# Output projection of both layers as one 2x2 block product over all heads, in a two-layer decoder trunk

## The chip, the cores and the metric

The kernel runs on one core of a Trainium2 chip. A core has five instruction queues that run at the same time and wait for each other through semaphores: TensorE (PE, with its weight loads shown as PEld), VectorE (DVE), ScalarE (ACT), GpSimd (POOL) and SyncE (SP), which issues the DMAs. The metric is the device time of one execution in microseconds (us); smaller is better.

## The reference, cut to what matters

One sequence of 1024 tokens, width 1024, float32. Layer A is a retention layer of 4 heads (query and key width 256, value width 512), layer C a stick-breaking attention of 8 heads (128, value width 256) whose keys and values come from layer A's output. In both, all heads' outputs, gated, are concatenated to 2048 columns and multiplied by one 2048 x 1024 matrix; that is the output projection.

```python
# layer A
o = retention_chunkwise(q, k, v)                    # per head: (1024, 512)
o = (o - mu) * rsqrt(var + EPS)                     # over each head's 512 columns
o = merge_heads(o) * silu(g)                        # (1024, 2048)
y = o @ ret_w_out[i]                                # output projection, 2048 x 1024
h = x + rms_norm(y, ret_norm_post[i])
k_shared, v_shared = split(rms_norm(h, kv_norm) @ w_kv)
# layer C
z = einsum('bhqd,bhkd->bhqk', qb, k) * scale
log_not = where(causal, log_sigmoid(-z), 0)
suffix  = cumsum(log_not, axis=3, reverse=True) - log_not
weights = where(causal, exp(log_sigmoid(z) + suffix), 0)
o = merge_heads(einsum('bhqk,bhke->bhqe', weights, v)) * silu(g)
y = o @ sb_w_out[j]                                 # output projection, 2048 x 1024
h = h + rms_norm(y, sb_norm_post[j])
```

## The kernel before

*Arithmetic.* Every float32 operand of a matmul is split into a high and a low part: `split` writes the high part with ScalarE (L514) and the rest with VectorE (L515). `mm3` (L410) makes one product from three matmuls, high by high, high by low, low by high (L413, L414, L415). In the rows the tile `whl` holds split weights, `wraw` and `vo` raw ones, `xh` (and `oT`, `qk`, `AT`, `ko`) split activations.

*Tiling.* The tokens are two halves `t` of 512. The input projections of both layers are 2x2 block products already: 7 products (numbers 1, 2, 5, 6, 7, 3, 4) of half-size blocks where the plain way has 8, with sums and differences of the operands made by VectorE. They are cut into pieces by the class `Phase`, and `merge` deals the pieces of one job out among the steps of another.

*Heads.* Layer A has eight turns (t, head), layer C eight pairs (t, two heads), each in two half heads; I number these n = 0 to 15, where 0 to 7 are the first token half and 8 to 15 the second. In attention `rows` makes the scores of a half head: for each of four blocks of 128 queries (in the second half in two parts, the keys of the other half and the own ones) three matmuls into a `pz` bank, two sigmoids by ScalarE into a tile `A` (even n; `xh` for odd n) and a tile `sgn` (L1275, L1276), two triangular selections by POOL on the diagonal block (L1280, L1281), a running product by VectorE over all keys (L1283) and a multiply (L1284). `mix` then takes each block of 128 keys: PE turns it (L1311, four transposes, one for each block of queries, from the four tiles `A`), ScalarE and VectorE split it to `AT`, and PE multiplies it with V into two `po` banks. The scores of half head n + 1 are dealt out among the steps of `mix` of half head n. A gate multiplies `po` (L1339).

*Output projection, head by head.* `outs` (L427) multiplies one head's four blocks `oT` by that head's strip of weights, two blocks of the contraction at a time, for each of 8 blocks of 128 output columns; the result lies with the columns on partitions, and each head adds its part to a running sum `ys` in SBUF (L452 for the first head, L455 later). In attention's second half `out_t` does the same with the tokens on partitions. A head's projection (16 pieces) is dealt out among the steps of the next head, or the next pair: in retention by the loop in `layer_a`, in attention by this one, with the last pair's in `finish`:

```python
for n in range(2, 16):
    A = heads[n // 2]
    if n % 2 == 0:
        pre, out = heads[n // 2 - 1].out(ys, ...)
    ...
    merge(A.mix(n % 2), (out[8 * (n % 2):][:8], 0 if n % 2 else 1, 1), (rows_of(n + 1), 0, 1), (extra, 1, 1))
```

The sums are then normalised (`a_post`, `c_post`, `finish`) and x or h is added; attention's split weights are prepared by `w_out` and kept in DRAM (`w_d`).

*Order.* The code above only says which step depends on which. `arrange` (L101) collects every instruction of the engines, works out a latest time for each, places them one after the other on a model of the engines with its own prices (`place`), repeats this from the back (`justify`), keeps the best of five, and ties each engine's queue to that order. Within PSUM there are four kinds of bank, `ma`, `mb`, `z` and `o`, two of each; of `sgn` there are 2 tiles, of `AT` 3, of `whl` 3.

Of the kernel before, what the change touches and what calls it, by code (L numbers as in the profile page):

```python
# [13 lines left out]
F32 = mybir.dt.float32  # L14
# [4 lines left out]
D = 1024  # L19
# [47 lines left out]

def _time(s, chip):
# [32 lines left out]
def arrange(nc, tc, tag_of, bufs, banks, turns):  # L101
# [4 lines left out]
    for ins in nc.cur_bb.bb.instructions:  # L106
# [10 lines left out]
        reads = [(b.tensor.name, _cells(b)) for b in s.ins if type(b.tensor).__name__ == "Tile"]  # L117
        writes = [(b.tensor.name, _cells(b)) for b in s.outs if type(b.tensor).__name__ == "Tile"]
# [3 lines left out]
        for name, m in writes:  # L122
            s.before |= {o.k for o, n, w in last[name] if n & m}
        for name, m in reads:
            last[name].append((s, m, False))
# [183 lines left out]
def trunk(ctx, tc, xT, wts, gains, trig, ident_in, cols, last_gain, x_late, out):  # L309
# [62 lines left out]

    warm = sb.tile([128, 8], F32, name="warm")
# [25 lines left out]
    def unit(idx, gain=None):  # L399

        w = S("whl", [2, 1024], F32R)
        for c in range(2):
            o = 512 * c
            raw = raw_w()
            dma(raw, wts[idx, :, o:o + 512])
            for a, b, g in [(p[0] - o, p[1] - o, p[2]) for p in gain if o <= p[0] < o + 512] if gain else [(0, 512, None)]:
                split((w[:, 0, o + a:o + b], w[:, 1, o + a:o + b]), raw[:, a:b], g)
        return w

# [6 lines left out]

    def ahead(n, make):

        box = {}

        def get(u):
            if u < n and u not in box:
                box[u] = make(u)
            return box.get(u)
        return get

    def outs(weights, oT, ys, tags, first, y_d=None, acc=None, kept=None):  # L427


        box = {}  # L430
        get = ahead(4, weights)

        def chunk(j):
            c, half = divmod(j, 2)
            ng, b = divmod(c, 2)
            w = get(ng)
            if j % 4 == LEAD:
                get(ng + 1)
            if half == 0:
                box["p"] = PS(banks4[c % 4])  # L440
                if b == 0 and first:
                    ys.append(S(tags[ng], [2, 512]))
                if b == 0 and kept is not None:
                    kept.append(S("v", [2, 512]))
            p, y = box["p"], ys[ng][:, b]
            for e in (2 * half, 2 * half + 1):
                n = slice(256 * e + 128 * b, 256 * e + 128 * b + 128)
                mm3(p[:], w[:, 0, n], w[:, 1, n], oT()[e][:, 0, :], oT()[e][:, 1, :], e == 0, e == 3)
            if half == 0:
                return  # L450
            if first:
                A_.activation(y, p[:], AF.Copy)  # L452
                return
            f = y if acc is None else kept[ng][:, b] if kept is not None else S("f2", [512])[:]
            V.tensor_tensor(f, p[:], y, ALU.add)  # L455
            if acc is not None:
                if kept is None:
                    dma(y_d[c], f)
                sumsq(acc, f, c)

        return [lambda: get(0)], [lambda j=j: chunk(j) for j in range(16)]
# [13 lines left out]

    def sumsq(acc, src, c):
        if c == 0:
            acc.append(S("acc", [512]))
            A_.activation(acc[0][:], src, AF.Square)
        else:  # L480
            t = S("f2", [512])
            A_.activation(t[:], src, AF.Square)
            V.tensor_tensor(acc[0][:], acc[0][:], t[:], ALU.add)
# [40 lines left out]
    turned = out[0:512, :].rearrange("a (b t) -> (a b) t", b=2)  # L524
    straight = out[512:1024, :]
    ht_d = dr.tile([1024, 512], F32, tag="ht", name="ht")
    st_d = [[dr.tile([128, 512], F32, tag=f"st{h}{d}", name=f"st{h}{d}") for d in range(2)] for h in range(NH)]
    y_d = [[dr.tile([128, 512], F32, tag=f"y{t}{c}", name=f"y{t}{c}") for c in range(8)] for t in range(2)]
    h_d = [[DRAM(f"h{t}{c}", F32) for c in range(4)] for t in range(2)]
# [4 lines left out]
    w_d = [[[DRAM(f"w{p}{n}{i}", F32R) for i in range(2)] for n in range(4)] for p in range(NPAIR)]  # L534
# [12 lines left out]
    B, tabs = Ctx(), []  # L547

    def a_open():
# [58 lines left out]
        def sums(i):  # L608
            if i == 0:
                L.sum = S("small", [4])  # L610
            w = S("ko", [1024])
            dma(w[:], x_late[128 * i:128 * i + 128, :])
            A_.activation(w[:], w[:], AF.Square, accum_out=L.sum[:, i:i + 1])

# [8 lines left out]
    class Ret:  # L623
# [3 lines left out]

        def out(self, ys, acc=None, kept=None):
            return outs(lambda ng: unit(self.base + 12 + ng), lambda: self.oT, ys, ("AT", "AT", "AT", "A"), self.h == 0,
                        y_d[0], acc, kept)  # L630
# [140 lines left out]
        def gate(self):  # L771
            o = S("qk" if self.n % 2 else "oT", [4, 2, 512], F32R)
            self.oT = [o[:, e] for e in range(4)]
# [11 lines left out]

            return [lambda ib=ib: step(ib) for ib in range(4)]

    def a_post(t, y_d, acc, kept=None):

        box = {}  # L790

        def stat1():
            box["col"] = rstd_col(acc[0])
# [910 lines left out]
```

## Time and profile before

| | |
|---|---|
| median of 3 runs | 1626.89 us (1626.64 to 1629.45) |
| profiled execution: span from the first instruction to the last | 1625.3 us |
| what the median has beside that span | 1.6 us |
| PE busy | 1615.8 us (99%) |
| DVE, ACT, POOL busy | 1220.5, 804.1, 124.2 us |
| moved by DMA | 392.72 MB, mean 242 GB/s |

A row of the timeline reads: start, duration, engine, source line, operation, output tile<-input tiles, partitions x columns, count; in brackets the idle time before it and what ended it. A row of the groups has count, total busy time, mean duration in ns, idle time. A DMA row has the size of one and the median time from its issue to its landing.

### The profile page before, as it was taken

What the parts mean: (1) busy time and instruction counts of PE and PEld (TensorE: products, weight loads), DVE (VectorE), ACT (ScalarE), POOL (GpSimd) and SP (SyncE); (2) the same over time, 40 slices, a digit from 0 to 9 for tenths busy, and PEclk for the clock granted to TensorE, in tenths of its full rate; (3) what the DMA queues carried; (4) which work ended last, traced back from release to release, by engine and by line L of the source; (5) the groups of instructions that cost most, each with busy time, mean ns of one, the idle gap of its engine ahead of it and who ended that gap; (6) DMA issues with size and microseconds to landing.
All of it is one profiled execution on the core that took longest, in us unless ns stands there. A gap on an engine that the chain in (4) does not pass through costs nothing.

```text
span 1625.3 us, 22472 instructions
## 1 busy us (share of the span) xinstructions
PE 1615.8 (99%) x7619; PEld 1348.1 (83%) x7619; DVE 1220.5 (75%) x1957; ACT 804.1 (49%) x1535; POOL 124.2 (8%) x271
## 2 busy tenths in 40 slices
PE   9999999999999999999999999999999999999998
PEld 7888888888888888888888888888888888888887
DVE  8897866654668888887689877767649567878776
ACT  8653334433356555544356665557644433554442
POOL 0000000000022212211000000000001111011110
PEclk9999999999999999999999999999999999999999
DMA  9757755543387878784786788988337988869783
GB/s 318 240 166 261 246 205 197 207 143 122 119 265 254 305 251 281 235 293 144 238 292 207 263 310 300 333 291 300 132 123 236 332 300 322 289 221 326 260 244 93
DMA packets 194834, 392.72 MB, mean 242 GB/s; under 512 B 34976, under 2 KB 51488, under 8 KB 192160
## 3 DMA queue, kind: packets, MB, share of 16 engines
q1 hardware_dynamic: 194000, 390.23, 69.9%
q8 instruction: 60, 0.98, 0.2%
q10 hardware_dynamic: 720, 1.07, 0.2%
q14 instruction: 54, 0.44, 0.1%
HBM read 268.01 MB, written 123.21 MB: 241 GB/s over the span
## 4 chain that ended last, share of the span: by engine, by line
PE 98%; DVE 1%; issue 0%; ACT 0%; DMA 0%; SPq 0%; DVEq 0%; POOLq 0%; POOL 0%
PE pma L413 12%; PE pma L414 12%; PE pma L415 12%; PE pmb L413 9%; PE pmb L414 9%; PE pmb L415 9%; PE po L414 6%; PE po L415 6%; PE po L413 6%; PE pz L415 3%; PE pz L414 3%; PE pz L413 3%; PE pz L1311 2%; PE pz L783 1%; DMA A<-in_xT_dram 0%
## 5 line engine op out<-in xcount | busy, mean ns | idle before, releaser
L515 DVE TENSOR_TENSOR whl<-wraw,whl 128x512 fp32r<-128x512 f32 x266 | 176.1, 686 | 88.6 <-ACT whl L514 86.0
L514 ACT ACTIVATE whl<-wraw 128x512 fp32r<-128x512 f32 x266 | 156.2, 625 | 171.2 <-issue 65.6
L1283 DVE TENSOR_TENSOR_SCAN sgn<-sgn 128x128 f32<-128x128 f32 (+3 forms) x64 | 86.6, 1354 | 16.9 <-POOL sgn L1281 16.7
L515 DVE TENSOR_TENSOR AT<-pz,AT 128x512 fp32r<-128x512 f32 (+1 forms) x96 | 51.2, 552 | 51.9 <-ACT AT L514 51.6
L514 ACT ACTIVATE AT<-pz 128x512 fp32r<-128x512 f32 (+1 forms) x96 | 45.0, 491 | 70.7 <-PE pz L1311 69.7
L413 PE MATMUL pmb<-oT,whl 128*128 128x512 f32 x192 | 75.9, 395 | 0.0
L415 PE MATMUL pmb<-oT,whl 128*128 128x512 f32 x192 | 75.3, 392 | 0.0
L414 PE MATMUL pmb<-oT,whl 128*128 128x512 f32 x192 | 75.2, 392 | 0.0
L413 PE MATMUL pmb<-qk,whl 128*128 128x512 f32 x184 | 72.4, 394 | 0.0
L415 PE MATMUL pmb<-qk,whl 128*128 128x512 f32 x184 | 72.2, 392 | 0.0
L414 PE MATMUL pmb<-qk,whl 128*128 128x512 f32 x184 | 71.8, 390 | 0.0
L515 DVE TENSOR_TENSOR whl<-vo,whl 128x512 fp32r<-128x512 f32 x62 | 41.7, 689 | 35.1 <-ACT whl L514 35.0
L897 ACT ACTIVATE f<-pma 128x512 f32<-128x512 f32 x52 | 30.8, 595 | 49.8 <-PE pma L415 49.4
L514 ACT ACTIVATE whl<-vo 128x512 fp32r<-128x512 f32 x62 | 37.5, 624 | 33.6 <-PE pma L415 17.1
L413 PE MATMUL pma<-xh,whl 128*128 128x512 f32 x136 | 53.3, 392 | 0.0
L415 PE MATMUL pma<-xh,whl 128*128 128x512 f32 x136 | 53.1, 390 | 0.0
L414 PE MATMUL pma<-xh,whl 128*128 128x512 f32 x136 | 53.1, 390 | 0.0
L1280 POOL TENSOR_SCALAR_AFFINE_SELECT A<-A 128x128 f32<-128x128 f32 x32 | 12.0, 376 | 534.8 <-ACT A L1275 534.8
L920 ACT ACTIVATE wraw<-wraw,gn 128x256 f32<-128x256 f32 x102 | 45.4, 497 | 8.7 <-DMA wraw<-in_wts_dram 8.6
L1275 ACT ACTIVATE xh<-pz 128x512 f32<-128x512 f32 (+3 forms) x48 | 23.6, 492 | 50.9 <-PE pz L415 50.7
L1276 ACT ACTIVATE sgn<-pz 128x512 f32<-128x512 f32 (+2 forms) x96 | 46.7, 488 | 0.0
L690 POOL TENSOR_SCALAR_AFFINE_SELECT sc<-sc 128x256 fp32r<-128x256 f32 x16 | 10.8, 692 | 447.6 <-DVE sc L515 447.4
(578 smaller groups left out, 5142.3 us busy)
## 6 DMA issues: line engine op xcount, KB each, us to landing
wraw<-in_wts_dram SPq DMA_DIRECT2D x332, 256.0 KB, 3.9
whl<-w SPq DMA_DIRECT2D x56, 512.0 KB, 5.9
vo<-in_wts_dram SPq DMA_DIRECT2D x70, 256.0 KB, 4.5
xh<-k SPq DMA_DIRECT2D x32, 512.0 KB, 6.7
v<-v SPq DMA_DIRECT2D x32, 512.0 KB, 5.4
k<-A SPq DMA_DIRECT2D x21, 512.0 KB, 5.3
e<-whl SPq DMA_DIRECT2D x10, 1024.0 KB, 6.8
whl<-e SPq DMA_DIRECT2D x10, 1024.0 KB, 6.6
```

The lines of the kernel that those rows point to most:

```text
L413: MM(p, lh, rh, start=start, stop=False, **kw)
L414: MM(p, lh, rl, start=False, stop=False, **kw)
L415: MM(p, ll, rh, start=False, stop=stop, **kw)
L514: A_.activation(dst[0], src, AF.Copy)
L515: V.tensor_tensor(dst[1], src, f32(dst[0]), ALU.subtract)
L783: nc.tensor.transpose(pt[:, 128 * e:128 * e + 128], on[:, 128 * e:128 * e + 128], ident[:])
L897: A_.activation(c[:], p[:], AF.Copy)
L920: A_.activation(x, x, AF.Copy, scale=gcol(self.gains[col], 2 * (2 * i + k) + c))
L1275: A_.activation(a[:, o:o + ww], p[:, :ww], AF.Sigmoid)
L1276: A_.activation(n[:, o:o + ww], p[:, :ww], AF.Sigmoid, scale=-1.0)
L1283: V.tensor_tensor_scan(n[:, :W][:, ::-1], n[:, :W][:, ::-1], n[:, :W][:, ::-1], 1.0, ALU.mult, ALU.bypass)
L1311: nc.tensor.transpose(p[:, 128 * tb:128 * tb + 128], self.A[hh][tb][:, c0:c0 + 128], ident[:])
```

## The change

The class `Out` replaces `outs`, `out`, `out_t`, `finish`, `a_post` and `c_post` in both layers (`oA`, `oC`). The gated outputs of each head, in plain float32 with the columns on partitions, are stored to DRAM (`o_d`) and loaded again. The 1024 x 2048 by 2048 x 1024 product is cut into 2x2 blocks: rows by token half, the contraction by heads 0-1 and 2-3 (pairs 0-1 and 2-3), columns by halves of 512. Seven products of 512 x 1024 by 1024 x 512 are made; `left` loads a strip of weights and of operands, takes the differences (VectorE) and splits; `chunk` multiplies; what two products share is summed on in the same PSUM bank (`over`). The sums and differences of the weights are made earlier (`prep`) and stored (`s_d`). Products 1 and 2 need only the first token half and are dealt out among later heads: in retention among turns 2 to 7, in attention two of their sixteen pieces in each of half heads 4 to 7 and one in each of 8 to 15. Products 6, 7, 4, 5, 3 need all heads and stand in one block after the last head, in retention at the start of `layer_c`. The tokens now lie on partitions, so `post` normalises rows; in layer A `turn` transposes the new h by PE (64 transposes) for the projections that follow. The running sums in SBUF, `w_out` and the old tail go. In `arrange`, a PSUM bank counts as one unit in the dependencies, and writes by one engine to neighbouring parts keep their order (`behind`).

```diff
-            def chunk(j):        # outs: head by head
-            for e in (2 * half, 2 * half + 1):
-                mm3(p[:], w[:, 0, n], w[:, 1, n], oT()[e][:, 0, :], oT()[e][:, 1, :], e == 0, e == 3)
-            V.tensor_tensor(f, p[:], y, ALU.add)
...
+        def left(self, n, u):
+            w = self.w[n, u] = S("whl", [2, 1024], F32R)
+            for k in range(2):
+                raw, cl = raw_w(), slice(512 * k, 512 * k + 512)
+                dma(raw, self.s_d[n][u][:, cl] if n in self.s_d else self.src(*{1: (0, 0), 2: (1, 0), 4: (1, 1)}[n], 2 * u + k))
+                split((w[:, 0, cl], w[:, 1, cl]), raw)
...
+            elif n == 6:
...
+                p, q, x = get(0, 0, self.tags[5][u]), get(1, 0, self.tags[7][u]), get(1, 1, self.tags[6][u])
+                V.tensor_tensor(p[:], q[:], p[:], ALU.subtract)
+                V.tensor_tensor(q[:], x[:], q[:], ALU.subtract)
+                V.tensor_tensor(x[:], x[:], p[:], ALU.subtract)
...
+        def chunk(self, n, kts, tbs):
+            over = {7: 6, 4: 6, 3: 5}
+            if n not in over and kts[0] == 0:
+                self.bank[n] = [PS(x) for x in (("o", "o", "z", "z") if n == 5 else banks4)]
+            banks = self.bank[over.get(n, n)]
+            for tb in tbs:
...
+                    mm3(banks[tb][:], a[:, 0, tl], a[:, 1, tl], w[:, 0, cl], w[:, 1, cl], n not in over and kt == 0, kt == 7,
+                        goes_on=n in over)
...
-            merge(A.mix(n % 2), (out[8 * (n % 2):][:8], 0 if n % 2 else 1, 1), (rows_of(n + 1), 0, 1), (extra, 1, 1))
-        last()
+            fill = outs.pieces(2 * n - 8, 2 * n - 6) if 4 <= n < 8 else outs.pieces(n, n + 1) if n >= 8 else []
+            merge(heads[n // 2].mix(n % 2), (fill, 0, 1), (rows_of(n + 1), 0, 1))
+        P = Phase([(oC, n) for n in (6, 7, 4, 5, 3)], ())
```

Over the program PE has 190 matmuls of 512 columns fewer (6467 to 6277), 24 fewer of 256, 20 fewer of one column, and 64 transposes of 128 more. VectorE has 1958 instructions for 1959, ScalarE 1623 for 1529, POOL 292 for 276, and SP issues 1242 DMAs for 1143.

Two places show how the queues change. The first is PE's queue at the end of the scores of half head 12, before the change; `pz_14294` is the last score, `A_14273` the tile that the engines make from it.

```order
L413 MATMUL pz_14294<-xh_14054,xh_14056 128x512
L414 MATMUL pz_14294<-xh_14054,xh_14056 128x512
L415 MATMUL pz_14294<-xh_14054,xh_14056 128x512
L1311 MATMUL pz_14328<-ident,A_14060 128x128
L1311 MATMUL pz_14328<-ident,A_14131 128x128
L413 MATMUL pma_14378<-whl_14323,qk_14016 128x512
L414 MATMUL pma_14378<-whl_14323,qk_14016 128x512
```

Between the last score and the first reading of `A_14273` stand 32 matmuls of the output projection (`whl`, `qk`):

```order
L413 MATMUL pma_14413<-whl_14451,qk_14016 128x512
L414 MATMUL pma_14413<-whl_14451,qk_14016 128x512
L1311 MATMUL pz_14328<-ident,A_14273 128x128
L1311 MATMUL pz_14338<-ident,A_14060 128x128
L1311 MATMUL pz_14338<-ident,A_14131 128x128
```

The same place in PE's queue after the change; the last score is `pz_13845`, its tile `A_13819`.

```order
L412 MATMUL pz_13845<-xh_13663,xh_13665 128x512
L413 MATMUL pz_13845<-xh_13663,xh_13665 128x512
L414 MATMUL pz_13845<-xh_13663,xh_13665 128x512
L414 MATMUL po_13688<-AT_13792,v_13552 128x128
L1286 MATMUL pz_13867<-ident,A_13669 128x128
L1286 MATMUL pz_13867<-ident,A_13723 128x128
L1286 MATMUL pz_13867<-ident,A_13782 128x128
L1286 MATMUL pz_13867<-ident,A_13819 128x128
L1286 MATMUL pz_13877<-ident,A_13669 128x128
L1286 MATMUL pz_13877<-ident,A_13723 128x128
```

The projection's rows are gone from between the score and the transposes.

The second place is the end of the last retention turn. Before, PE's last transposes of the head's normalised output (`sgn`) stood among the projection of the head before it, with the last head's own projection (`pma_7479<-qk`) behind:

```order
L415 MATMUL pmb_7437<-oT_6689,whl_7371 128x512
L783 MATMUL pz_7460<-ident,sgn_7332 128x128 x4
L413 MATMUL pmb_7437<-oT_6689,whl_7371 128x512
L414 MATMUL pmb_7437<-oT_6689,whl_7371 128x512
L415 MATMUL pmb_7437<-oT_6689,whl_7371 128x512
L413 MATMUL pmb_7437<-oT_6689,whl_7371 128x512
```

After, PE has this; `po_6635` is the last retention product, `sgn_6665` its normalised rows, `pma_6818` the first bank of product 6, `xh_6788` its first operand:

```order
L414 MATMUL po_6635<-A_6548,sc_6536 128x512
L718 MATMUL pz_6693<-ident,sgn_6605 128x128 x4
L413 MATMUL pmb_6000<-whl_6417,oT_6200 128x512
L414 MATMUL pmb_6000<-whl_6417,oT_6200 128x512
L412 MATMUL pmb_6001<-whl_6417,oT_6200 128x512
L718 MATMUL pz_6703<-ident,sgn_6665 128x128 x4
L413 MATMUL pmb_6001<-whl_6417,oT_6200 128x512
L414 MATMUL pmb_6001<-whl_6417,oT_6200 128x512
L718 MATMUL pz_6753<-ident,sgn_6665 128x128 x4
L412 MATMUL pma_6818<-whl_6762,xh_6788 128x512
```

and VectorE, from the statistics of `po_6635` on, this:

```order
L680 BN_STATS small_6654<-po_6635 128x6
L459 TENSOR_TENSOR whl_6762<-wraw_6767,whl_6762 128x512
L681 BN_AGGR small_6655<-small_6654 128x2
L459 TENSOR_TENSOR whl_6794<-wraw_6795,whl_6794 128x512
L683 TENSOR_SCALAR small_6658<-small_6655 128x1
L793 TENSOR_TENSOR S_6805<-ko_6807,S_6805 128x1024
L794 TENSOR_TENSOR ko_6807<-ko_6807,v_6803 128x1024
L714 TENSOR_TENSOR sgn_6665<-sgn_6665,sg_6750 128x512
L793 TENSOR_TENSOR S_6781<-AT_6783,S_6781 128x1024
L792 TENSOR_TENSOR v_6855<-A_6857,v_6855 128x1024
```

After the last row of the normalisation (L714) three subtractions, of which two are shown, and three more instructions stand on VectorE up to the one that completes `xh_6788`; they stand between the last normalisation and the first matmul of the block.

More of the change, by code (lines that the diff above doesn't have):

```diff
@@ L123, in arrange @@
             s.before |= {o.k for o, n, w in last[name] if n & m}
+            s.behind |= set([o.k for o, n, w in last[name] if w and o.eng == s.eng and _span(n) & _span(m)][-1:])
         for name, m in reads:
@@ L547, in trunk @@
     B, tabs = Ctx(), []
+    B.rows = [None, None]
     def a_open():
@@ L1523, in layer_a @@
         at[kq].append(lambda: ring.__setitem__(slice(None), ["wraw", "wraw", "wraw", "vo", "vo"]))
+        for k in range(8):
+            at[kq + (end - kq - 20) * k // 8].append(lambda k=k: oA.prep(k))
         heads = [Ret(t, h) for t in range(2) for h in range(NH)]
```

526 lines of the change are left out of this document (202 added, 324 removed).

## The prediction, before the changed kernel was run

> **What bounds the kernel now.** I read the head of the page first, then the busy time by stretches, then the timeline at the places where the change takes work away.
>
> ```profile
> span 1625.3 us, 22472 instructions
> PE 1615.8 (99%) x7619; PEld 1348.1 (83%) x7619; DVE 1220.5 (75%) x1957; ACT 804.1 (49%) x1535; POOL 124.2 (8%) x271
> PE 98%; DVE 1%; issue 0%; ACT 0%; DMA 0%; SPq 0%; DVEq 0%; POOLq 0%; POOL 0%
> ```
>
> The third line is the chain that ended last: 98% of it is TensorE. A busy PE need not be one at its pace, so the pace comes from successive starts:
>
> ```profile
> 1494.98 0.39 PE L413 MATMUL pmb<-whl,qk 128*128 128x512 f32 x1
> 1495.21 0.39 PE L414 MATMUL pmb<-whl,qk 128*128 128x512 f32 x1
> 1495.44 0.39 PE L415 MATMUL pmb<-whl,qk 128*128 128x512 f32 x1
> ...
> 1616.04 0.28 PE L413 MATMUL pmb<-A,qk 128*128 128x256 f32 x1
> 1616.16 0.28 PE L414 MATMUL pmb<-A,qk 128*128 128x256 f32 x1
> ```
>
> A 512-column matmul costs 0.227 us of path (0.23 from start to start, though each is listed as 0.39 long), a 256-column one 0.12. The stretches (width, then busy time of PE, PEld, DVE, ACT, POOL where it works, then granted clock, DMA share, GB/s) show that PE never waits in the middle, and how much room the others have:
>
> ```profile
> 800.00:1000.00 200.00, 199.98 (x885) 164.83 (x884) 171.86 (x280) 118.45 (x228) 1.01 (x1) 1.00 0.78 275
> 1200.00:1400.00 200.00, 200.00 (x1025) 169.92 (x1025) 141.66 (x224) 86.31 (x195) 27.32 (x76) 1.00 0.81 283
> 1400.00:1590.00 190.00, 190.00 (x1000) 160.86 (x1000) 148.06 (x184) 89.60 (x187) 20.56 (x53) 1.00 0.81 267
> ```
>
> In attention (the last two) PE is full and VectorE at 71 to 78%. So PE work that goes is worth its full time, as long as what is left still covers the chains of the other engines. That is where the question lies: the work removed is the very work that PE does while those chains run.
>
> **The change part by part.** *Matmuls.* Seven products for eight on 1536 matmuls of 512 columns is 192 fewer; the two orders give 190 fewer, with 24 fewer of 256 columns, 20 fewer of one column and 64 more 128-column transposes (the turn of h). 190 x 0.227 = 43.1; 24 x 0.12 = 2.9; the one-column ones about 2. A transpose costs about 0.1: four stand between 1289.68 and 1290.04 in the rows below, so 64 cost 6 to 7. Sum: **-41 us**. VectorE issues one instruction fewer, ScalarE 94 more at 0.6 us or less, POOL 16 more; all beside PE. SP issues 99 DMAs more; whether they cost anything hangs on the few that somebody waits for, below.
>
> *Attention, second token half.* Half head n+1 makes its scores while half head n multiplies. From the last score runs a chain: two sigmoids, two selections on POOL, the scan, a multiply; only then can PE turn that tile. In the profile it looks so (from half head 11 to 12):
>
> ```profile
> 1489.58 0.39 PE L415 MATMUL pz<-xh,xh 128*128 128x512 f32 x1
> ...
> 1490.01 0.60 ACT L1275 ACTIVATE A<-pz 128x512 f32<-128x512 f32 x1
> ...
> 1490.51 0.59 ACT L1276 ACTIVATE sgn<-pz 128x512 f32<-128x512 f32 x1
> ...
> 1490.68 1.22 POOL L1280 TENSOR_SCALAR_AFFINE_SELECT A<-A 128x128 f32<-128x128 f32 x1 [2.94 <-ACT A L1275]
> ...
> 1491.85 0.74 POOL L1281 TENSOR_SCALAR_AFFINE_SELECT sgn<-sgn 128x128 f32<-128x128 f32 x1
> ...
> 1492.62 2.29 DVE L1283 TENSOR_TENSOR_SCAN sgn<-sgn 128x1024 f32<-128x1024 f32 x1 [0.19 <-POOL sgn L1281]
> ...
> 1495.41 1.22 DVE L1284 TENSOR_TENSOR A<-A,sgn 128x1023 f32<-128x1023 f32 x1
> ...
> 1497.48 0.71 PE L1311 MATMUL pz<-ident,A 128*128 128x128 f32 x5
> ...
> L1280 POOL TENSOR_SCALAR_AFFINE_SELECT A<-A 128x128 f32<-128x128 f32 x32 | 12.0, 376 | 534.8 <-ACT A L1275 534.8
> ```
>
> The score is out at 1489.81, A is ready at 1495.41 + 1.22 = 1496.63: 6.8 us, with a slow POOL and another VectorE instruction in between. Bare (0.2 to the first sigmoid, 0.5, 0.59, 0.38 for a POOL selection by the mean in the last row, 2.29, 1.22) it is 5.2. PE turned the tile at 1497.48 and lost nothing, since 32 output-projection matmuls, 7.5 us, stood in between. In the new order they are gone: ahead of half heads 10, 11, 12 and 14 the last score stands at most one row ahead of the transposes, four rows ahead of the one that reads its tile, 0.4 us of work (the order rows shown with the change are those of half head 12, before and after). Ahead of 13 and 15 it is 4.7 and 2.3 us, ahead of 8 and 9 there is 6.2 and 8.0. With a chain of 6.3, between the two ends: 4 x 5.9 + 1.6 + 4.0 = 29 (bare: 4 x 4.8 + 0.5 + 2.9 = 23).
>
> Behind it comes a second one, from the transposes over ScalarE's copy to the first product with V:
>
> ```profile
> 1284.77 0.39 PE L415 MATMUL pz<-xh,xh 128*128 128x512 f32 x1
> ...
> 1287.08 1.18 DVE L1283 TENSOR_TENSOR_SCAN sgn<-sgn 128x512 f32<-128x512 f32 x1
> ...
> 1288.30 0.69 DVE L1284 TENSOR_TENSOR xh<-xh,sgn 128x511 f32<-128x511 f32 x1
> ...
> 1289.68 0.60 PE L1311 MATMUL pz<-ident,xh 128*128 128x128 f32 x4
> 1289.99 0.98 ACT L514 ACTIVATE AT<-pz 128x512 fp32r<-128x512 f32 x2 [1.10 <-PE pz L1311]
> ...
> 1290.82 0.40 PE L413 MATMUL po<-AT,v 128*128 128x512 f32 x1
> ```
>
> 1289.68 to 1290.82 is 1.1 us; in the new order only four more transposes (0.4) and at times one matmul cover it: about 0.5 at each of eight boundaries, **4 us**. Together **33 us** for the second half; 27 to 38.
>
> *Attention, first half.* These rows give the shorter chain as well: 1285.00 to 1288.99, 4.0 us. The new order leaves 3.6, 3.8, 1.0 and 2.7 us of PE work ahead of half heads 2 to 5 and 5.5 or more at the others: 0.4 + 0.2 + 3.0 + 1.3 = 5, and some 3 for the second chain. **8 us**; 3 to 10.
>
> *The end of the retention layer.* The old kernel ended with the last head's projection, 96 matmuls, behind the last retention products. Now the block of products 6, 7, 4, 5, 3 needs every head. The last head's normalisation takes
>
> ```profile
> 734.92 0.70 DVE L744 BATCH_NORM_STATS2 small<-po 128x6 f32<-128x512 f32 x1 [0.59 <-PE po L415]
> 738.66 0.69 DVE L779 TENSOR_TENSOR sgn<-sgn,sg 128x512 f32<-128x512 f32 x1 [1.12 <-ACT sgn L763]
> L648 DVE TENSOR_TENSOR S<-S,tab 128x1024 f32<-128x1024 f32 x16 | 19.7, 1230 | 0.2
> L515 DVE TENSOR_TENSOR xh<-S,xh 128x512 fp32r<-128x512 f32 x32 | 21.7, 691 | 2.9 <-ACT xh L514 2.7
> v<-v SPq DMA_DIRECT2D x32, 512.0 KB, 5.4
> ```
>
> 4.4 us; in VectorE's new order two weight splits and two 1024-wide subtractions stand inside it, which makes 5.7, and PE has 2.0 us of work ahead of the transposes: 3.7. Product 6 then waits for three more subtractions of 1.23 and three instructions of 0.69, 5.8 us less some 1.0 that lies beside the transposes: 4.8. The third and fourth strips of its operand are stored by the last head and loaded again, two landings of 5.4, two subtractions, a split, some 15 us after the transposes; the stalls so far and 36 matmuls cover 12: about 3. **12 us**, 8 to 17; beyond this the block has PE ahead of VectorE.
>
> *The end of attention.* The same round trip, from the last product with V over the gate, store, load, two subtractions and a split: 0.7 + 10.8 + 2.5 + 1.3 + 1.3 of VectorE rows standing between = 16.6 us, against some 13 us of matmuls on the strips that are there: **4 us**, 2 to 8.
>
> *The rest.* In retention the projection's work thins out while VectorE (86% busy in 800 to 1000) keeps its own: it comes to about 95% of PE's work by a count of both orders, with 3 us or more of cover at each chain: **3 us**, 0 to 8. The last block ends with a full 512-column half where the old one ended with a quarter:
>
> ```profile
> 1618.44 0.28 PE L415 MATMUL pma<-A,qk 128*128 128x256 f32 x1
> ...
> 1620.75 1.42 DVE L1421 SCALAR_TENSOR_TENSOR AT<-AT,col,xh 128x512 f32<-128x512 f32 x2 [0.66 <-POOL col L1418]
> ```
>
> 6.6 us now from the end of PE to the span's end; the add and the square on 512 instead of 256 columns cost some 0.3 to 0.6 more each: **1 us**.
>
> *Does a stall also slow what follows?* The only idle PE that the trace shows is at the start:
>
> ```profile
> 1.71 4.21 PE L386 MATMUL pz<-f,onesr 128*128 128x512 f32 x9 [1.71 <-DVE f L384]
> ...
> 6.57 0.63 PE L415 MATMUL pma<-whl,oT 128*128 128x512 f32 x1
> 7.00 0.63 PE L413 MATMUL pma<-whl,oT 128*128 128x512 f32 x1
> ...
> 8.29 0.39 PE L414 MATMUL pmb<-whl,oT 128*128 128x512 f32 x1
> 8.52 0.39 PE L415 MATMUL pmb<-whl,oT 128*128 128x512 f32 x1
> ```
>
> Until about 7.8 the pace is 0.43 to 0.47, then 0.23: 6.1 us at half speed, 3.0 lost. A stall in mid kernel may cost between nothing and that; no row shows one, and the stalls here are shorter than a cold start, so the sum takes nothing and the rival below the rest. The Trainium skill ("TensorE: Matmul & The Clock Gate", Part 1: The HAM clock gate) says that an idle window of about 3.4 us puts TensorE back to half rate, until it has been busy for about as long again; it would add some 1.7 us for each stall of over 5 us, an estimate from that page, some 7 us on the four longest.
>
> **The sum.** -41 + 33 + 8 + 12 + 4 + 3 + 1 = **+20 us**. The profiled execution has 1625.3 of span, 1.6 below the median of 1626.9; the same 1.6 around it gives 1646.9, **1647**, 1.2% slower. With all stalls at their low ends it is -41 + 27 + 3 + 8 + 2 + 0 + 1 = 0, at their high ends -41 + 38 + 10 + 17 + 8 + 8 + 1 = +41.
>
> **The rivals.**
> - *The stalls with their clock.* Each of the four longest stalls, and perhaps the three of about 4 to 5 us, is followed by a cold start of up to 3.0 us: 12 to 21 on top, **1659** at four. For it speaks the start of the trace; against it, that nothing shows how short an idle time suffices.
> - *Faster: only the four long stalls are real.* Waiting PE lets ScalarE, POOL and VectorE run ahead, so that the next chain starts with no queue. If each runs at its bare length and the shorter covers suffice, there remain 4 x 4.8 at the four boundaries, 3 at half head 15, 4.8 for the start of the first block, 1 for the tail: 28, so 1627 - 41 + 28 = **1614**. It decides once stalls total under 41. Against it: the four boundaries have no cover in the order itself, and VectorE is the engine with the least room.
> - *The round trips.* Product 6 alone loads 12 operands of 512 KB, 4 stored sums and 8 strips of weights of 256 KB, 9.4 MB for 96 matmuls (21.8 us): 430 GB/s if none came earlier, where the busiest stretch above has 283. If the loads queue up, 5.4 becomes 10 and each layer's end costs 8 to 10 more: **1665**.
> - *Gain and stalls cancel*: 1627, all low ends at once.
>
> **How the numbers follow.** About 0.2% (3 us) is what a measurement of this kernel tells from none. Forecast 0.53 (its own range 1632 to 1655); clock 0.18; round trips 0.08; faster 0.14; cancelled 0.07. The range, 1610 to 1666, takes in the faster case's and the round trips' centres and leaves out their outer parts. Faster 0.14, same 0.07, slower 0.79.
>
> **What would show it.** Right: PE idle of 4 to 6 us in front of the transposes at half heads 10, 11, 12 and 14, released by VectorE's multiply; PE busy some 40 us lower; idle PE at the start of both blocks behind VectorE subtractions and DMA. The clock: a pace of 0.43 behind these stalls. Wrong: a first transpose that runs within 3 us of the last score, or PE idle of less than 25 us in attention.

## The result

The changed kernel takes 1706.87 us (median of 4 runs, 1702.47 to 1710.32) against 1627.64 us beside it: 1.0486 times as long, interval 1.0465 to 1.0508. That is 79 us slower; forecast were 20, with a range up to 1666.

The head of its page and the third line, the chain that ended last:

```profile
span 1707.8 us, 22505 instructions
PE 1621.5 (95%) x7429; PEld 1332.7 (78%) x7429; DVE 1261.9 (74%) x1956; ACT 858.4 (50%) x1656; POOL 145.0 (8%) x287
PE 86%; DVE 6%; issue 3%; DMA 2%; ACT 2%; POOL 0%; SPq 0%; DVEq 0%; POOLq 0%; ACTq 0%
```

Span and mean granted clock of before:

```profile
core 0: 1625.3 us, clock 0.999
```

and of after:

```profile
core 0: 1707.8 us, clock 0.970
```

PE is busy 6 us longer, with 190 matmuls fewer. Its idle time (span less busy) went from 9.5 to 86.3 us: +77. The mean clock loses (1 - 0.970) x 1707.8 = 51 us of the span, but not all of that is PE's work. The trace's record of the granted clock has 15 spells at half rate (0.50) up to the last matmul; half of each spell is lost, 36 us while PE was busy and 12 while it stood idle anyway; 3 more lie behind the last matmul. In the kernel before, the record has no half rate up to the last matmul (it begins some 5 to 8 us into the span in both, so the slow start that the prediction shows is not in it).

One more correction makes the sum. A matmul is listed 0.39 long for 0.23 of path, so ahead of each wait PE counts as busy a little longer than it works: 66 gaps of over 0.02 us in place of 4, some 13 us (an estimate from the starts). Taken from start to start, the change is: work -44, waits +90 (77 idle and the 13), half-rate clock +37 (36 by the record); together 83, and the spans differ by 82.5. The sum has to close, since the work is what is left of it; what bears it out is that the -44 comes close to the prediction's own count of the matmuls, -41.

By stages (width, busy time of PE, PEld, DVE, ACT, POOL, granted clock, DMA share, GB/s):

```profile
370.00:385.00 15.00, 12.83 (x50) 10.03 (x49) 8.39 (x14) 2.30 (x4) 0.00 (x0) 0.89 0.98 334
440.00:677.00 237.00, 226.75 (x1136) 184.88 (x1135) 180.89 (x314) 133.82 (x267) 74.70 (x125) 0.99 0.89 316
677.00:700.00 23.00, 14.84 (x53) 10.51 (x52) 21.71 (x28) 13.14 (x25) 2.84 (x3) 0.78 0.98 351
1250.00:1365.00 115.00, 105.22 (x551) 89.41 (x550) 86.56 (x140) 57.90 (x132) 23.02 (x63) 0.94 0.87 302
1365.00:1563.00 198.00, 162.00 (x782) 129.83 (x780) 141.64 (x156) 91.83 (x196) 22.36 (x58) 0.88 0.67 226
1563.00:1610.00 47.00, 38.98 (x159) 30.80 (x160) 35.29 (x46) 16.91 (x29) 0.00 (x0) 0.83 0.52 178
1610.00:1698.00 88.00, 88.00 (x390) 72.88 (x389) 59.00 (x96) 32.19 (x60) 4.23 (x7) 1.00 0.43 141
```

Read the difference between the width and PE: 10.3 us idle in the retention turns, 8.2 at the start of the first block, 9.8 in attention's first half, 36 in its second, 8.0 at the start of the last block; the rest of that block runs full. And read the clock: below 1 only where PE idles, 0.88 over 198 us in the second half, where 17 of the 36 us are lost.

A boundary in attention's second half, into half head 10 (the prediction shows the one into 12, before):

```profile
1419.15 0.39 PE L414 MATMUL pz<-xh,xh 128*128 128x512 f32 x1
...
1419.44 0.42 PE L1286 MATMUL pz<-ident,A 128*128 128x128 f32 x2
...
1420.24 1.08 POOL L1255 TENSOR_SCALAR_AFFINE_SELECT A<-A 128x128 f32<-128x128 f32 x1 [1.45 <-ACT A L1250]
...
1421.73 1.08 DVE L1259 TENSOR_TENSOR A<-A,sgn 128x895 f32<-128x895 f32 x1
...
1422.73 2.28 DVE L1258 TENSOR_TENSOR_SCAN sgn<-sgn 128x1024 f32<-128x1024 f32 x1
1422.87 0.48 PE L1286 MATMUL pz<-ident,A 128*128 128x128 f32 x1 [3.01 <-DVE A L1259]
1425.05 1.22 DVE L1259 TENSOR_TENSOR A<-A,sgn 128x1023 f32<-128x1023 f32 x1
...
1426.33 1.33 PE L1286 MATMUL pz<-ident,A 128*128 128x128 f32 x5 [2.98 <-DVE A L1259]
...
1428.87 0.63 PE L413 MATMUL pz<-ko,xh 128*128 128x512 f32 x1
1429.29 0.63 PE L414 MATMUL pz<-ko,xh 128*128 128x512 f32 x1
...
1432.10 0.39 PE L414 MATMUL po<-AT,vo 128*128 128x512 f32 x1
1432.34 0.39 PE L412 MATMUL po<-AT,vo 128*128 128x512 f32 x1
```

PE waits 3.01 and 2.98 us (the brackets) for VectorE's multiply of the third and of the fourth tile; then the five transposes take 1.33 where five took 0.71 before, and the matmuls start 0.42 apart, listed 0.63 long, until about 1431.9. Then 0.24 again. The view of waits sums up who released PE (line waited for, total, times, longest):

```profile
PE pz L1286 <- DVE A L1259: 23.4, 9, 3.4
PE pz L1286 <- DVE xh L1259: 15.4, 5, 5.5
PE pma L412 <- ACT xh L458: 8.5, 4, 3.2
PE pz L718 <- DVE sgn L714: 5.0, 3, 4.2
```

39 us wait for that multiply; the other two rows are waits for operands of the block products and for retention's normalised rows.

### The profile page after: what moved, and what is told of

Same layout as the page of the kernel before. It is cut to its first block, busy times and chain, and to the rows that moved or that the text cites. A ratio compares the mean times of both kernels' runs of the same rounds, so it can differ in the third digit from the quotient of the medians.

```text
span 1707.8 us, 22505 instructions
## 1 busy us (share of the span) xinstructions
PE 1621.5 (95%) x7429; PEld 1332.7 (78%) x7429; DVE 1261.9 (74%) x1956; ACT 858.4 (50%) x1656; POOL 145.0 (8%) x287
## 4 chain that ended last, share of the span: by engine, by line
PE 86%; DVE 6%; issue 3%; DMA 2%; ACT 2%; POOL 0%; SPq 0%; DVEq 0%; POOLq 0%; ACTq 0%
PE pma L414 10%; PE pma L413 10%; PE pma L412 10%; PE pmb L412 7%; PE pmb L413 7%; PE pmb L414 7%; PE po L412 7%; PE po L413 6%; PE po L414 6%; PE pz L412 4%; PE pz L413 4%; PE pz L414 4%; PE pz L1286 2%; DVE sgn L1258 2%; PE pz L718 1%
## 5 line engine op out<-in xcount | busy, mean ns | idle before, releaser
L458 ACT ACTIVATE whl<-wraw 128x512 fp32r<-128x512 f32 x310 | 183.1, 626 | 220.1 <-PE pmb L414 90.5
L459 DVE TENSOR_TENSOR whl<-wraw,whl 128x512 fp32r<-128x512 f32 x310 | 205.4, 689 | 110.8 <-ACT whl L458 108.4
L459 DVE TENSOR_TENSOR AT<-pz,AT 128x512 fp32r<-128x512 f32 (+1 forms) x96 | 51.7, 552 | 51.5 <-ACT AT L458 51.1
L412 PE MATMUL pma<-whl,xh 128*128 128x512 f32 x112 | 46.0, 414 | 8.7 <-ACT xh L458 8.5
L1286 PE MATMUL pz<-ident,A 128*128 128x128 f32 x144 | 30.2, 319 | 24.0 <-DVE A L1259 23.4
L414 PE MATMUL pma<-whl,xh 128*128 128x512 f32 x112 | 46.2, 415 | 4.2 <-DVE xh L459 4.2
L1286 PEld LDWEIGHTS pz<-ident,A 128*128 128x128 f32 x144 | 20.6, 163 | 32.2 <-DVE A L1259 24.0
L413 PE MATMUL pma<-whl,xh 128*128 128x512 f32 x112 | 45.5, 406 | 0.0
L412 PE MATMUL pmb<-whl,xh 128*128 128x512 f32 x112 | 44.9, 401 | 0.0
L413 PE MATMUL pmb<-whl,xh 128*128 128x512 f32 x112 | 44.8, 400 | 0.0
```

What stands on the lines that cost most here:

```text
L412: MM(p, lh, rh, start=start, stop=False, **kw)
L413: MM(p, lh, rl, start=False, stop=False, **kw)
L414: MM(p, ll, rh, start=False, stop=stop, **kw)
L458: A_.activation(dst[0], src, AF.Copy)
L459: V.tensor_tensor(dst[1], src, f32(dst[0]), ALU.subtract)
L1286: nc.tensor.transpose(p[:, 128 * tb:128 * tb + 128], self.A[hh][tb][:, c0:c0 + 128], ident[:])
```

## The experiments

Idle is span less PE busy, from each run's own profile. The last column is half of the time that PE was busy at half rate, by the trace's record of the clock. (Span times one minus the mean clock would be 2 to 16 us more, since it counts the half rate while PE stands idle and behind the last matmul too.)

| run | median us | ratio to before (interval) | idle us | lost at half rate while busy us |
|---|---|---|---|---|
| before | 1627 | 1 | 9.5 | 0 |
| after | 1706.9 | 1.0486 (1.0465 to 1.0508) | 86.3 | 36 |
| e0_arrange | 1627.4 | 0.9998 (0.9989 to 1.0007) | 9.6 | 0 |
| e1_warm | 1699.8 | 1.0445 (1.0430 to 1.0461) | 56.8 | 17 |
| e2_shift | 1702.1 | 1.0461 (1.0443 to 1.0478) | 81.1 | 31 |
| e3_nochain | 1642.5 | 1.0087 (1.0072 to 1.0102) | 47.5 | 7 |
| e3b_nochain_before | 1631.0 | 1.0019 (1.0009 to 1.0028) | 11.7 | 0 |
| e_aonly | 1641.3 | 1.0083 (1.0066 to 1.0100) | 31.2 | 7 |
| e_conly | 1698.4 | 1.0428 (1.0412 to 1.0445) | 64.9 | 31 |
| e4_ownfirst | 1662.4 | 1.0221 (1.0197 to 1.0246) | 58.5 | 17 |
| e5b_nofill | 1707.6 | 1.0496 (1.0480 to 1.0512) | 87.7 | 31 |
| e5_banks | 1654.2 | 1.0168 (1.0150 to 1.0186) | 51.1 | 16 |
| e6_both | 1656.5 | 1.0181 (1.0166 to 1.0196) | 57.5 | 12 |
| e7_conly_banks | 1642.3 | 1.0097 (1.0082 to 1.0112) | 32.1 | 11 |
| e8_conly_spread | 1634.9 | 1.0048 (1.0033 to 1.0063) | 30.5 | 6 |
| e9_aonly_nofill | 1660.5 | 1.0202 (1.0181 to 1.0224) | 44.3 | 10 |

### Which part of the change

The scheduler's new dependencies alone, in the kernel before:

> The kernel before with only the changed dependencies of the scheduler (a PSUM bank as one unit, writes of neighbouring parts in order). All theories: 1627 within 3 us; if it is 5 or more above, part of the loss is the scheduler's and not the projection's.

1627.4: neutral in the kernel before; in the changed kernel they were not taken out. Then one layer at a time (`Out` for `oA` only, or `oC` only; the other layer keeps the old code).

> Block product in the retention layer alone; attention's output projection head by head as before. The final residual adds x in place of h (same transfers), so its output is not the reference's. Theory 1 (each layer pays for its own lost cover): work -22, idle 20 and half-rate clock about 15 as the trace shows them up to 700 us: about 1627 + 13 = 1640. Rival (layer A's part is cheap, the loss is attention's): 1627 - 22 + 12 = about 1617. Rival (layer A's new layout of h and its store and load spoil attention): above 1660.

> Block product in the attention layer alone; retention's projection head by head as before. The final residual adds x in place of h (same transfers). Theory 1: work -22, idle 60 (53 in attention, 6 in the last block), half-rate clock some 35: about 1627 + 70 = 1697, so that the two halves add up to the whole change (79). Rival (the two layers disturb each other): the two sums differ from 79 by over 15.

+14 and +71 against before; the whole change is +79. So the layers' losses nearly add, and attention has five sixths of them.

### The clock by itself

The stream of `e_gate` holds PE up by one VectorE instruction of a set width between two runs of matmuls:

```diff
+            MM(q[:], w[:], x[:], start=True, stop=True)
+            V.tensor_tensor(pad[:, :n], pad[:, :n], q[:, 0:1].broadcast_to([128, n]), ALU.max)
+            V.tensor_tensor(x[:, 0:16], pad[:, n - 16:n], pad[:, n - 16:n], ALU.max)
+            for _ in range(44 + 5 * j):
+                MM(p[:], w[:], x[:], start=True, stop=True)
```

> Not the reference's computation: a stream of 512-column matmuls of constants, held up 36 times by VectorE work of twelve lengths, three times each at shifting moments; it measures the clock by itself, and its total time means nothing. Theory 1: behind a wait of about 3.4 us or more always a spell of half rate of about 3.4 us or more (0.43 from start to start), 1.7 us lost; behind waits of 1 us or less none; between them now and then, by where a window falls. Rival 1 (any wait slows): spells behind waits of 0.5 us too. Rival 2 (only long idle slows): none below 5 us.

Its timeline, the runs of matmuls behind seven waits (in brackets):

```profile
194.25 12.55 PE L39 MATMUL p<-x,w 128*128 128x512 f32 x54 [0.99 <-DVE x L37]
...
337.55 13.01 PE L39 MATMUL p<-x,w 128*128 128x512 f32 x49 [1.79 <-DVE x L37]
...
352.57 12.53 PE L39 MATMUL p<-x,w 128*128 128x512 f32 x54 [1.79 <-DVE x L37]
...
393.64 12.53 PE L39 MATMUL p<-x,w 128*128 128x512 f32 x54 [2.05 <-DVE x L37]
...
439.45 14.15 PE L39 MATMUL p<-x,w 128*128 128x512 f32 x54 [2.59 <-DVE x L37]
...
473.23 11.41 PE L39 MATMUL p<-x,w 128*128 128x512 f32 x49 [3.65 <-DVE x L37]
...
488.51 14.09 PE L39 MATMUL p<-x,w 128*128 128x512 f32 x54 [3.66 <-DVE x L37]
```

54 matmuls take 12.5 us, or 14.1 behind some waits, 49 take 11.4 or 13.0: 1.6 lost, once per spell. It happened behind none of the 24 waits up to 1.52 us, one of three of 1.79, none of three of 2.06, all three of 2.59, two of three of 3.65 (the 49 in 11.41 us ran at full pace). So it is a matter of when the wait falls, as theory 1 had it, but from 1.8 us on. The Trainium skill ("TensorE: Matmul & The Clock Gate", Part 1: The HAM clock gate) has a free-running window of about 3.4 us, idle for a whole one; waits of 2.6 us suffice here, so a window need not be idle throughout.

The record of the clock says what does decide. In each trace all its changes within the kernel stand on one grid of 3.41 us, and whether a window runs at half rate goes by how long PE was busy in the window before. Three windows of `e_gate` and two of the changed kernel (width, PE busy and the rest as in the stages above, without ACT in `e_gate`):

```profile
437.28:440.69 3.41, 1.24 (x5) 1.05 (x6) 2.08 (x2) 0.00 (x0) 1.00 0.00 0
468.00:471.41 3.41, 1.57 (x7) 0.95 (x6) 1.80 (x1) 0.00 (x0) 1.00 0.00 0
471.41:474.82 3.41, 1.59 (x7) 1.33 (x8) 1.73 (x2) 0.00 (x0) 1.00 0.00 0
537.60:541.01 3.41, 1.75 (x6) 1.16 (x7) 2.90 (x5) 2.93 (x5) 0.69 (x2) 1.00 1.03 417
541.01:544.42 3.41, 3.41 (x9) 2.64 (x8) 1.10 (x3) 0.00 (x0) 0.00 (x0) 0.50 1.03 401
```

The first was followed by half rate (the matmuls at 439.45 above), and so was the fourth (the last row, 0.50); the second and the third were not: the wait of 3.65 that cost nothing had fallen half into each of them. Over all 17 traces 106 windows at full rate were followed by one at half rate. In 105 of them PE was busy for 1.95 us or less; in the other, at the start of `e_aonly`, for 2.68, of which eight one-column matmuls are listed with 0.95. A window with less than 1.57 was always followed by half rate. Full rate came back only behind a window with 2.94 or more, so a spell goes on as long as waits follow. So the limit is about half a window of work, however many waits the rest is made of: at 541 the changed kernel fell to half rate behind waits of 1.40 and 0.42. One wait of 2.17 did it here:

```profile
376.61 0.50 PE L412 MATMUL pmb<-qk,whl 128*128 128x512 f32 x1 [2.17 <-ACT whl L458]
...
378.57 0.63 PE L412 MATMUL pmb<-qk,whl 128*128 128x512 f32 x1
378.99 0.63 PE L413 MATMUL pmb<-qk,whl 128*128 128x512 f32 x1
...
380.65 0.39 PE L414 MATMUL pmb<-qk,whl 128*128 128x512 f32 x1
380.88 0.39 PE L412 MATMUL pmb<-qk,whl 128*128 128x512 f32 x1
```

Then in the kernel itself, work for PE that covers nothing:

```diff
                 p = PS("z")
+                for _ in range(KEEP.get(8 * self.t + 2 * self.pr + hh, 0) if i == 0 else 0):
+                    MM(p[:], onesr[:], onesr[:, 0:1].broadcast_to([128, 512]), start=True, stop=True)
                 for tb in range(t0, 4):
```

> Changed kernel, with 8 to 26 matmuls of constants (512 columns, result overwritten) ahead of the first transposes of half heads 10 to 15, where PE idles; they cover no chain, they only keep PE busy, about as long as it idles now (26 x 0.227 = 5.9 us). Theory 1 (idle PE slows its own clock: of the 79 us lost, about 50 are matmuls at half rate after waits): the waits stay, their time turns from idle to busy, but the half-rate spells behind them (2 to 3 us lost each at five places, 1.3 at one) go: 1707 - 13 = about 1694, granted clock up from 0.97. Theory 2 (the low clock comes from somewhere else, from load or from DMA): no spell goes, 1707 within 3 us. Theory 3 (dummy work delays the transposes): above 1710.

```profile
1469.17 5.93 PE L1287 MATMUL pz<-onesr 128*128 128x512 f32 x26
...
1476.05 0.76 PE L1289 MATMUL pz<-ident,A 128*128 128x128 f32 x5 [0.63 <-DVE A L1260]
...
1478.18 0.39 PE L414 MATMUL pz<-ko,xh 128*128 128x512 f32 x1
1478.41 0.40 PE L415 MATMUL pz<-ko,xh 128*128 128x512 f32 x1
```

The wait shrinks to 0.63 and full pace follows: the spell is gone. PE does 167 more matmuls (38 us; 32 of them stand ahead of half heads 4, 5 and 8, which the expectation does not name) and the kernel is 7 us faster, with 30 us less idle and 18 less at half rate: 38 - 30 - 18 = -10, as the spans of the two profiled executions have it (1707.8 to 1698.2). That is theory 1. That 13 were expected has two sides: 8 us of the dummies took no idle time away (at half head 8 a wait of 3.13 stays behind them), and the half rate fell by 5 more than the 13.

### What PE waits for in attention

Without the scan and the multiply behind it:

```diff
-                    V.tensor_tensor_scan(n[:, :W][:, ::-1], n[:, :W][:, ::-1], n[:, :W][:, ::-1], 1.0, ALU.mult, ALU.bypass)
-                    V.tensor_tensor(a[:, :W - 1], a[:, :W - 1], n[:, 1:W], ALU.mult)
```

> Changed kernel without the running product and the multiply of attention (the scan and the instruction after it on VectorE; the weights are the sigmoids alone, so the output is not the reference's). From the last score to the tile remain two sigmoids and one selection, some 1.5 us, with 0.3 to 1.8 us of cover. Theory 1 (the waits in attention are this chain, and the half-rate clock there follows them): idle in attention from 53 to about 15, each too short for a spell: 1707 - 38 - 33 = about 1636. Rival (PE waits for V, K or a bank, or the clock is low in attention for its load): idle or the spells stay, above 1665.

> The same two instructions taken from the kernel before. Theory 1: there the chain is hidden by the projection, so nothing changes: 1627 within 2 us. Rival (VectorE's share slows something): 1620 or less.

1642.5 from 1706.9, with 39 us less idle and 29 less at half rate, while the kernel before does not gain (1631, even 3 us slower, more than the 2 allowed for; its new order has one wait of 1.2, the cause of the rest I did not look for). With its chain the changed kernel takes some 64 us more than without, and the old one no more. The edit also takes 123 us of work off VectorE, so by itself it does not tell a late chain from a VectorE that is too busy; the run with own banks below does, which leaves that work in.

The filler moved to where the waits are longest:

```diff
-            fill = outs.pieces(2 * n - 8, 2 * n - 6) if 4 <= n < 8 else outs.pieces(n, n + 1) if n >= 8 else []
+            fill = outs.pieces(2 * n - 16, 2 * n - 14) if n >= 8 else []
```

> Changed kernel with the 16 pieces of products 1 and 2 in attention given two to each half head from 8 on, none to 4 to 7. By the work that its order leaves between the last score and the transposes of its tile, against 6.4 us in the second token half and 4.4 in the first (what the changed kernel's waits and covers add up to): waits of 6.1 at half head 8, 3.6 at 11 and 12, 5.4 at 14, 2.6 at 15, none at 9, 10 and 13, some 21 instead of 31; in the first half 3.1, 2.5, 2.5, 2.5 at 4 to 7, 3 to 4 more than now. Theory 1 (cover decides, the clock follows the waits over about 1.8 us): idle down by some 6 and as many waits long enough for a spell as now: 1707 - 4 = about 1703. Rival (how much filler lies in the second half decides): twice the filler there, 22 us more work beside the chains, 1707 - 20 = about 1687.

1702.1, 1703 expected: twice the filler in the second half bought 5 us, not much more than the changed kernel scatters (1702 to 1710). Waits went from one boundary to another, as the covers in its order had it: 5.9 us at half head 8, 7.1 at 14, none at 9, 10 and 13.

The chain made shorter, with the same result (own keys first, the scan carried on to the other half's by its start value):

```diff
-                o, KK, ww = (0, box["Ko"], 512) if self.t and part == 0 else (off, K, w)
+                own = part == 0
+                o, KK, ww = (off, K, w) if own else (0, box["Ko"], 512)
...
+                else:
+                    V.tensor_tensor_scan(n[:, :off][:, ::-1], n[:, :off][:, ::-1], n[:, :off][:, ::-1], n[:, off:off + 1], ALU.mult, ALU.bypass)
+                    V.tensor_tensor(a[:, :off], a[:, :off], n[:, 1:off + 1], ALU.mult)
...
-            blocks = ([(0, s) for s in range(4)] if self.t else []) + [(1, s) for s in range(4)]
+            blocks = [(1, s) for s in range(4)] + ([(0, s) for s in range(4)] if self.t else [])
```

> Changed kernel, same result by a shorter chain: in the second token half the own keys are scored, scanned and multiplied first (512 columns), the other half's keys after them with the scan carried on, and PE turns the own blocks first, so that from the last own score to the tile it is some 4.4 us (as in the first token half) and no longer 6.4. The order leaves 1.4 us of cover at half head 8, 2.1 at 12, 0.9 at 14, 1.2 at 15 (ahead of the remaining multiplies), 4.1 or more at the others: waits of 3.0, 2.3, 3.5 and 3.2, some 12 in place of 31. Theory 1 (the chain's length against its cover, and the clock behind it): idle -20, half-rate clock -15: 1707 - 35 = about 1672. Rival (PE then waits for the second part of the tile, VectorE being the bound of a half head): the waits move into the half head, 1695 or more.

1662.4: 44 us won, 28 of idle and 19 at half rate, 10 more than expected. Two microseconds less chain at each of eight boundaries are 16, and fewer waits are long enough for a spell; where the rest of the idle time went is not shown.

### Why the last score comes so late

The scores and the transposes share two `z` banks. First a control without any projection work in the second half, then the same with the scores in the banks that this leaves free:

```diff
-                p = PS("z")
+                p = PS(("ma", "mb")[tb % 2] if self.t else "z")
                 mm3(p[:, :ww], Q[:, 0, ql], Q[:, 1, ql], KK[:, 0, :ww], KK[:, 1, :ww], True, True)
```

> Changed kernel with product 2 of attention moved from the second token half into the last block: no projection work is left in half heads 8 to 15. The control of the next run. Theory 1: covers 1.7 at half head 10 and 0.4 at 11 to 15, waits of 4.7 and five times 6.0, 35 against 31, and the last block unchanged: 1707 + 5 = about 1712. Rival (the filler delays the chain): faster than 1700.

> The run before with one more edit: the scores of half heads 8 to 15 go to the banks ma and mb, which are free there, in place of the two z banks that they share with the transposes. Theory 1a (the last score comes late because scores and transposes queue for two z banks; with its own banks the next half head's scores stand ahead of this one's transposes): a half head is then bound by VectorE's some 18 to 20 us, no longer by 26.7: 4 us less each, idle -32 and half the spells of the second half gone: 1712 - 45 = about 1667. Rival 1b (the last score is late for the two sgn tiles, or for VectorE): within 10 us of the run before.

> Both edits together (own banks for the scores and own keys first). Theory 1: they remove the same waits, since with its own banks a half head is bound by VectorE, whose work stays: about 1665, no more than 10 us below the better of the two. Rival (two separate causes): they add up, 1635 or less.

The same 100 us of the three kernels, from half head 10 on, in the columns of the stages above: after, control, own banks.

```profile
1410.00:1510.00 100.00, 79.47 (x384) 63.64 (x383) 68.78 (x78) 46.02 (x98) 11.35 (x30) 0.85 0.63 211
1410.00:1510.00 100.00, 76.80 (x365) 61.16 (x364) 64.80 (x70) 42.42 (x90) 11.59 (x30) 0.83 0.60 203
1410.00:1510.00 100.00, 98.45 (x556) 83.61 (x556) 94.82 (x106) 58.69 (x129) 25.94 (x40) 1.00 0.84 291
```

The control is as slow as the change (1707.6): the filler in the second half was worth nothing. With own banks PE is 98% busy and VectorE 95%, with no projection work beside them, and the kernel takes 1654.2: 53 us from one edit, 13 more than theory 1a gave. Each half head's scores now run while the one before it is still multiplied, so its chain is done in time; here are the last score of a half head, VectorE's last multiplies for it (two in the row), and PE's transposes:

```profile
1449.10 0.40 PE L414 MATMUL pmb<-xh,xh 128*128 128x512 f32 x1
...
1460.40 2.31 DVE L1259 TENSOR_TENSOR xh<-xh,sgn 128x1023 f32<-128x1023 f32 x2
...
1463.57 0.82 PE L1286 MATMUL pz<-ident,xh 128*128 128x128 f32 x6
```

Between score and transposes PE has 14 us of attention's own work, where the changed kernel had 0.4, and it does not wait. So the shared banks are the cause of the late scores. One thing stays open: `arrange` gives out the banks of one kind in the order in which the code asks for them, so a score cannot pass a transpose that is asked for earlier. No run tells that rule from the mere number of two banks. Both edits together (1656.5) bring no more than the banks alone, as theory 1 has it: both take away the same waits. That VectorE is what bounds the half heads then is read from its 95% and no run tests it.

### What is left

> Attention's block product alone (retention's projection head by head, the final residual adds x in place of h), with product 2 in the last block and the scores of half heads 8 to 15 in the free banks. Theory 1 (the two layers' losses add, and the banks were the larger part of attention's): 1654 less the 14 of the retention layer alone = about 1640, against 1698 without the two edits. Rival (the edits repaired something that both layers share): 1655 or more.

> The run before with the last pieces of the gate's input projection, which fill half heads 0 and 1, spread over half heads 0 to 3. In the first token half no projection is left ahead of half heads 2 and 3, and TensorE waits there. Theory 1 (cover decides): about 5 us less than the run before, some 1635, and not yet below the kernel before, since the first half's chains stay short of work. Rival (VectorE alone bounds these half heads): no change.

> Retention's block product alone (final residual adds x), with products 1 and 2 moved from the heads into the block behind them: no projection work lies beside the retention turns. PE's work is the same as with the retention layer alone. Theory 1 (here too the projection was the cover of the turns' chains, and what idles is slowed afterwards): 43 us of filler less beside chains, idle up by some 20 in the turns and down by the wait at the layer's end, a few us more at half rate: 1641 + 20 = about 1661. Rival (the layer's loss is the block's start and its transfers, the turns are bound elsewhere): 1641 or less, since more work stands in the block to hide its loads.

1642.3, 1634.9 and 1660.5: within 2 us of theory 1 each time. The banks' gain is attention's own; in its first token half projection work spread over four half heads instead of two gives 7 us; in retention taking the filler away costs 19. No version beats the kernel before: the nearest, attention alone with the banks and the spread filler, is 0.5% slower, and retention, whose waits (22 us idle and 7 at half rate, against some 20 us of matmuls saved) no run mended, adds 14.

## Why the prediction was wrong

- *Matmuls, -41*: -44 from start to start. Right.
- *Attention, second half, 33*: 36 to 38. The waits of 5.9 forecast ahead of 10, 11, 12 and 14 were 6.0, 6.0, 6.0 and 5.7, released by the multiply. Ahead of 15 there were 5.5 for 4.0, and 2.3 more for an operand of the block, ahead of 8 2.0 for nothing. Right, and the marks named for it are there.
- *Attention, first half, 8*: 9.8. *End of the retention layer, 12*: 8.2. *End of attention, 4*: 6.1 of the 8.0 above (the rest belongs to the 2.3 just named). Right in kind and about in size; the extra 8 to 10 us that the rival of the round trips put at each layer's end did not come.
- *Retention, 3*: 10.3, and 2.2 more at 374 where new weight sums delay a strip of weights. Mis-sized: "3 us or more of cover at each chain" held for the chains looked at, not for the filler, which now waits for its own operands. *Tail, 1*: 2.5. The waits together are 77 of idle time, or 90 with the listed ends of the matmuls ahead of them, for 61: 29 too little.
- *"A stall in mid kernel may cost between nothing and that; ... the sum takes nothing"*: this is the step that failed. It cost 37 us. The start of the trace showed half pace and its price (3.0), and the rule of the Trainium skill's page stood beside it, but I took it for a rival with four to seven events. There were 15 spells of one to three windows, 28 windows in all, because about half a window without work is enough: waits of about 2 us do it, and this change makes 18 of 1.8 us or more. With 37 in place of 0, 90 in place of 61 and 3 us more of work saved, +20 becomes +83, the measured 82.5 between the profiled executions.
- *The range*: it treated the clock as an alternative to the sum (1659) and not as a part of its upper end. Stalls at their high ends and the rival's own 21 us together would have been 1689; with the 37 measured, 1705.
- The cause behind the waits went deeper than "the cover is gone". The cover hid that scores and transposes queue for two banks; with own banks the same half heads need no cover (`e5_banks`).

## What to carry to other kernels

Work that a saving takes off the bounding engine may be the work that hides the other engines' chains; count, boundary by boundary, what is left in the queue between a chain's start and its end, and price each wait with the slow clock behind it, not with its own length alone. Where a chain starts too late, look for what holds its first instruction back (here a bank) before giving it more cover or making it shorter: that edit, once the filler had been taken out of these banks at no cost, won back 53 of 79 us.

## What the hardware showed that I had not expected

The granted clock changes on a grid of 3.41 us. Half rate followed when PE had been busy for about half of a window or less (under 1.57 us it always did, over 1.95 never, but for the one case named above), full rate only behind a window busy for 2.94 or more. So single waits of 1.8 to 2.6 us can cost 1.6 us more, one of 3.65 did not, and shorter ones do it when two fall into one window (1.40 and 0.42). Where waits follow each other every 20 to 30 us the loss at half rate reaches nearly half of the idle time itself (36 us on 77). POOL's selection of 128 columns takes 0.29 us alone, and 0.29 also at 1421.28, beside a VectorE instruction that reads a PSUM bank; it took 1.08 at 1420.24, beside the running product, whose operands all lie in SBUF.
